# The first expert's choice as a job of its own, the sorting in three pieces, the last block's gathers first

## The chip, the cores and the metric

The kernel runs on one core of a Trainium2 chip. The metric is the device time of one execution in microseconds, as the median of the runs shown. The engines are PE (TensorE's matmuls), DVE (VectorE), ACT (ScalarE), POOL (GpSimd) and SP (SyncE, which issues most of the DMAs). Each works through its own queue of instructions in the order in which the program emits them.

## The reference

One layer of a decoder block on 1024 tokens of width 1024, in float32. A mixer (stick-breaking attention and a gated linear recurrence, each projected, gated and merged, then an output projection), a layer norm, a mixture of experts, and a layer norm again:

```
h = layer_norm(alpha * x + mixer(x))              # the mixer ends in merged @ w_out
logits = h @ router_w + router_b                  # 32 experts
top 4 of 32 for each token, gates = softmax of the four
per expert: hcat = h_rows @ w_up[e] + b_up[e]     # 1024 -> 2048, even columns gate, odd linear
            act = min(glu, 7) * sigmoid(1.702 * glu) * (clip(lin, -7, 7) + 1)
            y = act @ w_down[e] + b_down[e]       # 1024 -> 1024
out = layer_norm(alpha * h + sum over the four of gate * y)
```

Only the rows that chose an expert go through it. Which rows these are is known when all 1024 tokens have been routed.

## The kernel before

Products that must keep float32 accuracy are done as three matmuls on a high and a low part of each operand (`split` makes the parts: ACT casts the high one, DVE or POOL subtracts for the low one). The kernel projects the input, runs the recurrence and the attention, merges both branches, and then comes to the part that the change touches, `outproj` and the start of `experts`.

**`outproj`** works on eight blocks (tb) of 128 tokens. `project` (L955) multiplies a block of the merged branches by `w_out`, which lies in the slots `raw0` to `raw5`, `wh0`, `wl0`, `wh1`, `wl1`: 48 matmuls in two halves into two PSUM banks called `mix`. `add` (L948) adds the residual for a half and takes its statistics; after both halves `layer_norm` (L890) makes h of the block on DVE, in four instructions of 512 columns, and h is stored to `h_scratch`. `route(tb)` (L1049) does the block's routing in pieces, each ending in a `yield`: transposes of h (L1057) and their copies on ACT, the router product (L1064), the logits and the top four and gates on DVE (L1069 to L1108), `spread` (L1099, the gates over the 32 experts), then `place` (L983: how many earlier tokens chose each expert, a running sum `macc` in L989), the row numbers (L1117 to L1123), four indirect DMAs on POOL that write token and gate into the table `tab_scratch` (L1130), then the biases' product with the gates (L1148 to L1160), whose result is stored as the start of the accumulator.

The order is written out by hand. A loop (L1169 to L1183) goes through the pieces of `project`, two of the eight products of a half at a time; each piece is a step. After each step, every routing job in `live` makes one piece. Blocks 0 and 1 take 16 steps together, later ones 8 each; a block's routing begins `LAG` = 5 steps after its projection. The last two pieces of block 7 have no step.

**The first expert** does not wait for the full routing. After block `CHOOSE` = 4, `choose` (L1011) takes the expert with the fewest tokens so far, keeps its number in `e0` (by which SP loads its weights) and marks which tokens of the blocks so far chose it, as 128 by 128 squares S of zeros and ones (`chosen`, L996). After block 5 `fetch_chosen` (L1034) makes the token numbers from S (L1040) and gathers these rows of h from `h_scratch` by an indirect DMA (L1046). The rows of blocks 6 and 7 are added on PE: `gather` (L1005) multiplies h by S into the two banks `x0`, on top of the fetched rows, so that the first expert's input stands there transposed, never having gone through memory. `choose` and `fetch_chosen` are called inside `route` by `yield from`, so that the block's own scatters come behind them.

**The tail** (L1185 to L1211) brings routing of blocks 6 (`side`) and 7 (`last`) to their ends in an order of its own, with `until(g, what)` running one up to a named point: m is the mask of a block, s its squares, x its gather, g its gates, p its scatters. `sort_experts` (L1233) counts each expert's tokens and sorts the experts by them, giving `eid`, the list by which all further weights are loaded.

**`experts`** (L1607) runs the 32 experts. Each piece of an expert's two products has a weight load (SP, into one of six `raw` slots of 1 MB), a `part` (the split into one of eight `wh`, `wl` pairs; every fifth is POOL's) and the matmuls. Loads are emitted `RLOOK` = 14 pieces ahead and parts `LOOK` = 6 ahead. The first expert multiplies its first 512 columns whole (L1524, from the copy `xf` of its input in `wh5`), its others in parts (L1511). What is left of the routing stands in the list `side`, up to two pieces for each piece of the first expert. Expert 1's rows are gathered by POOL (L1354) after `enter` has loaded its places; PE transposes them (L1390) at the first piece of expert 1. `bank` (L168) gives the PSUM banks in turn, four `mix` and two `sm`. Experts whose capacity is over 128 are wide (18 of them), the others narrow (14).

`scratch` (L232) runs early and fills the DRAM scratch, the rows of `h_scratch` with zeros that no store has reached when they are read.

Of the kernel before, what the change touches and what calls it, by code (L numbers as in the profile page):

```python
# [42 lines left out]
LAG = 5  # L43
HOLD = 3
STILL = 2
CHOOSE = 4
POOLED = 5
ORD = (("s", 0), ("s", 1), ("s", 2), ("s", 3), ("s", 4), ("c", 0, 2, "p"), ("a", 0, "pp", "pp"), ("s", 5), ("s", 6), ("a", 1, "pp", "pp"), ("c", 2, 6, "v"), ("s", 7), ("c", 6, 8, "v"), ("a", 2, "xx", "xx"), ("a", 3, "xx", "vv"), ("a", 4, "pv", "vv"), ("a", 6, "pp", "pv"), ("a", 5, "vp", "vv"), ("a", 7, "vp", "vv"))
LOOK = 6
# [98 lines left out]
class Block:  # L148
# [19 lines left out]
    def bank(self):  # L168

        i = self.turns.get("bank", 0)  # L170
        self.turns["bank"] = (i + 1) % 6
        return self.fps.tile([128, 512], F32, name="mix" if i < 4 else "sm", bufs=4 if i < 4 else 2)

    def dram(self, name, shape, dtype=F32):
        return self.nc.dram_tensor(name, shape, dtype).ap()
# [56 lines left out]
    def scratch(self):  # L232

        nc = self.nc
        self.tab_d = self.dram("tab_scratch", (NE * ROWS, 2), I32)
        self.h_d = self.dram("h_scratch", (ROWS, D))
        self.acc_d = self.dram("acc_scratch", (ROWS, D))
        n = NE * ROWS // 128
        for i in range(2):
            t = self.work.tile([128, n], I32, name="E0", bufs=EBUFS[0])  # L240
            nc.sync.dma_start(t, self.a["c_tab"][:, n * i:n * i + n])
            nc.gpsimd.dma_start(self.tab_d.rearrange("(p r) c -> p (r c)", p=128)[:, n * i:n * i + n], t)
        z = self.work.tile([128, 512], F32, name="E0", bufs=EBUFS[0])
        nc.gpsimd.memset(z, 0.0)
        for d in (self.h_d, self.acc_d):
            for half in range(2):
                nc.gpsimd.dma_start(d[T:T + 128, 512 * half:512 * half + 512], z)

        for half in range(2):
            nc.gpsimd.dma_start(self.h_d[T - 128:T, 512 * half:512 * half + 512], z)  # L250


    def load_x(self):
# [636 lines left out]
    def layer_norm(self, pool, r, st, g, b, out):  # L890

        nc = self.nc
        mv = pool.tile([128, 2], F32, name="mv", bufs=2)
        nc.vector.bn_aggr(mv, st)
        y = self.rsqrt(pool, mv[:, 1:2], 1.0, LN_EPS, 1)
        for op0, k, op1, v, to in ((OP.subtract, mv[:, 0:1], OP.mult, g, r), (OP.mult, y, OP.add, b, out)):
            for half in range(2):
                s = slice(512 * half, 512 * half + 512)
                nc.vector.scalar_tensor_tensor(to[:, s], r[:, s], k, v[:, s], op0=op0, op1=op1)

    def outproj(self):
# [53 lines left out]
        def project(tbs):  # L955

            for tb in tbs:
                W["ps", tb] = [self.fps.tile([128, 512], F32, name="mix", bufs=4) for _ in range(2)]
                W["r", tb] = self.residual[:, tb % 2]
            todo = [(tb, half, k) for tb in tbs for half in range(2) for k in range(KT)]  # L960
            if len(tbs) > 1:
                todo.sort(key=lambda x: x[2])
            for i, (tb, half, k) in enumerate(todo):
                mh, ml = (p[k // 4][:, k % 4, 128 * (tb % 2):128 * (tb % 2) + 128] for p in self.mt[tb // 2])
                n = slice(512 * half, 512 * half + 512)
                o = W["ps", tb][half]
                wh, wl = self.wo[k]
                nc.tensor.matmul(o, mh, wh[:, n], start=k == 0, stop=False)
                nc.tensor.matmul(o, mh, wl[:, n], start=False, stop=False)
                nc.tensor.matmul(o, ml, wh[:, n], start=False, stop=k == KT - 1)  # L970
                if k == KT - 1:
                    add(tb, half)
                    if half and tb + 2 < NB:
                        load_x(tb + 2)
                if i % 2 and i + 1 < len(todo) or i + 2 == len(todo):
                    yield
            for tb in tbs:
                h = self.at(HSLOTS[tb], [128, D], F32)
                self.layer_norm(lk, W["r", tb], W["st", tb], ln_g, ln_b, h)
                nc.gpsimd.dma_start(self.h_d[128 * tb:128 * tb + 128], h)  # L980
                W["h", tb] = h

        def place(tb, m):  # L983

            pr = self.fps.tile([128, 512], F32, name="sm", bufs=2)
            nc.tensor.matmul(pr[:, :NE], self.before, m, start=True, stop=False)
            nc.tensor.matmul(pr[:, :NE], self.ones, macc, start=False, stop=True)
            nc.vector.scalar_tensor_tensor(mr[:, tb], pr[:, :NE], 1.0, m.bitcast(F32), op0=OP.add, op1=OP.mult)
            nc.vector.tensor_add(macc, macc.bitcast(F32), m.bitcast(F32))  # L989
            if tb > CHOOSE + 1:  # L990
                chosen(tb, tb + 1)
                yield "s"
                gather(W["h", tb], S[tb], False, tb == NB - 1)
                yield "x"
# [15 lines left out]

        def choose():  # L1011

            yield
            ps = self.fps.tile([128, 512], F32, name="sm", bufs=2)
            nc.tensor.matmul(ps[:, :NE], self.ones, macc, start=True, stop=True)
            neg = wk.tile([128, NE], F32, name="lg", bufs=2)
            nc.vector.tensor_scalar(neg, ps[:, :NE], -1.0, None, op0=OP.mult)
            mx = wk.tile([128, 8], F32, name="mx", bufs=2)
            mi = wk.tile([128, 8], U32, name="mi", bufs=2)
            nc.vector.max(mx, neg)  # L1020
            nc.vector.max_index(mi, mx, neg)
            ef = wk.tile([128, 4], F32, name="idf", bufs=2)
            nc.vector.tensor_copy(ef, mi[:, :4])
            nc.vector.tensor_scalar(oe, self.iota_e, ef[:, :1], None, op0=OP.is_equal)
            self.e0 = self.epool.tile([1, 1], I32, name="e0")
            nc.vector.tensor_copy(self.e0, ef[:1, :1])
            self.ch0 = self.epool.tile([128, 1], F32R, name="ch0")
            nc.vector.memset(self.ch0[2 * NE:].bitcast(F32), 0.0)
            nc.vector.tensor_scalar(self.ch0[:2 * NE], self.ecol, ef[:2 * NE, :1], None, op0=OP.is_equal)
            self.squares = self.at("wl2", [128, NB, 128], F32)  # L1030
            chosen(0, CHOOSE + 1)
            yield

        def fetch_chosen():  # L1034

            chosen(CHOOSE + 1, CHOOSE + 2)
            yield
            ps = self.fps.tile([128, 512], F32, name="sm", bufs=2)
            for tb in range(CHOOSE + 2):
                nc.tensor.matmul(ps[:, :2], S[tb], self.tokf[:, tb:tb + 2], start=tb == 0, stop=tb == CHOOSE + 1)  # L1040
# [8 lines left out]
        def route(tb):  # L1049
            h = W["h", tb]  # L1050
            hT = self.at("wl4", [128, D], F32).rearrange("p (k t) -> p k t", t=128)
            for g in range(2):
                last = tb == NB - 1
                p = self.fps.tile([128, 512], F32, name="mix" if last else "ht", bufs=4 if last else 2)
                p = p.rearrange("p (k t) -> p k t", t=128)
                for i in range(4):
                    nc.tensor.transpose(p[:, i], h[:, 128 * (4 * g + i):128 * (4 * g + i) + 128], self.idn)  # L1057
# [64 lines left out]
            idx = wk.tile([128, 4], I32, name="idx", bufs=2)  # L1122
            nc.vector.tensor_copy(idx, ds_)  # L1123
            if tb == CHOOSE:
                yield from choose()
            if tb == CHOOSE + 1:
                yield from fetch_chosen()
            for k in range(4):
                nc.gpsimd.memset(self.spacer, 0.0)
                s = nc.gpsimd.indirect_dma_start(  # L1130
# [4 lines left out]
                scat.append(s)  # L1135
            if late:
                yield "p"
                if tb == NB - 1:
                    self.sort_experts(oe)
                    yield "o"  # L1140
                spread()
            else:
                for _ in range(HOLD):
                    yield
# [42 lines left out]
        def until(g, what):  # L1187
            while next(g) != what:
                pass
# [1 line left out]
        side = live.pop()  # L1191
        next(side)
        until(side, "m")
        next(last)
        self.x0 = [self.fps.tile([128, 512], F32, name="mix", bufs=4) for _ in range(2)]
        gather(self.xg[0], self.idn, True, False)
        next(last)
        until(side, "s")
        until(last, "m")
        until(side, "x")  # L1200
        until(last, "s")
        until(last, "x")
        yield
        for g in (side, last):
            until(g, "g")
            until(g, "p")
        yield
        until(last, "o")
        yield
        for g in live + [side, last]:  # L1210
            yield from g  # L1211


# [19 lines left out]
    def sort_experts(self, first):  # L1233
# [2 lines left out]
        ps = self.fps.tile([128, 512], F32, name="sm", bufs=2)  # L1236
        nc.tensor.matmul(ps[:NE, :NE], self.ones[:, :NE], self.macc, start=True, stop=True)
        nc.tensor.matmul(ps[:NE, 32:34], self.macc, self.ones[:, :2], start=True, stop=True)

        key = cp.tile([NE, NE], F32, name="key")  # L1240
        nc.vector.scalar_tensor_tensor(key, ps[:NE, :NE], 32.0, c32[:, 0], op0=OP.mult, op1=OP.add)
# [10 lines left out]
        nc.vector.tensor_reduce(pos, key, axis=AX.X, op=OP.add)  # L1252
        perm = cp.tile([NE, NE], F32, name="perm")
        nc.vector.tensor_scalar(perm, c32[:, 3], pos, None, op0=OP.is_equal)
        ps = self.fps.tile([128, 512], F32, name="sm", bufs=2)
        for i in range(2):
            nc.tensor.matmul(ps[:1, 32 * i:32 * i + 32], ec[:, i:i + 1], perm, start=True, stop=True)
# [349 lines left out]
    def experts(self, routing):  # L1607
# [76 lines left out]
            call(t)  # L1684
        fetch(10)
        next(routing)
        next(routing)
        nc.gpsimd.memset(self.xg[1], 0.0)
        for i in range(LOOK):
            part(i)  # L1690
        soon, side, listing = [], [], None
        side += [("r", lambda: next(routing, None))] * 28

        def due(ts):

# [4 lines left out]

        for i, (q, kind, j) in enumerate(order):
            part(i + LOOK)
            fetch(i + RLOOK)
            if kind == "down" and j == 0:
                due([t for t in soon if t[1] == q])
            if kind == "up" and j == 0 and q:
# [274 lines left out]
```

## Time and profile before

| | |
|---|---|
| median of 3 runs | 2585.21 us (2582.81 to 2588.27) |
| profiled execution | 2587.85 us |
| its span, first to last instruction | 2586.3 us |
| mean granted TensorE clock | 0.972 |
| PE, PEld | 94%, 84% of the span busy |
| DVE, ACT, POOL | 72%, 58%, 34% |
| DMA | 551.18 MB, mean 213 GB/s |

The projection of the output and the routing run from about 875 to 1034 us, the first expert from 1043, and the experts up to about 2500. In the rows below a line number is that of the kernel, a tile's name is that of the place it lies in (a small routing tile carries the name of the slot it is cut from: `aTA`, `gl`, `yT`, `wl`). An engine's idle time before an instruction stands in brackets with what ended it. The granted clock is 1.00 at 2.4 GHz and 0.50 at 1.2 GHz, and a stretch's mean lies between.

### The profile page before, as it was taken

To read this page: it belongs to the slowest core of one execution; us is meant where nothing else is said; L and a number is where in the kernel's file an instruction comes from. 1 tells how busy PE (TensorE), PEld (TensorE's weight loads), DVE (VectorE), ACT (ScalarE), POOL (GpSimd) and SP (SyncE) were. 2 spreads that over 40 slices of the span, in tenths; PEclk is the share of its full clock that TensorE was granted. 3 is DMA by queue.
4 is the path that set the end of the run, shared out by engine and by line. 5 is a ranking of instruction groups with operands and counts; after the bars stand their busy time and mean duration, and the time that the engine had idled before them with its cause. 6 is when DMAs were issued, how large, how long until landed. Compare 5 with 4: busy or idle time off the path is not lost. (4 is left out here: it accounts for less than half of the span.)

```text
span 2586.3 us, 42032 instructions
## 1 busy us (share of the span) xinstructions
PE 2438.3 (94%) x15521; PEld 2177.2 (84%) x15521; DVE 1865.0 (72%) x3160; ACT 1491.7 (58%) x2558; POOL 878.0 (34%) x751
## 2 busy tenths in 40 slices
PE   8999999989979987799999999999999999999992
PEld 8898888887867765599999999999899899899892
DVE  3216674338884575688878788988888888889885
ACT  3213332327664311477777777777777777777772
POOL 1011011004331232344444443444444444454443
PEclk9999999999989998899999999999999999999996
DMA  5321243223324524789899899997999989999963
GB/s 164 107 80 56 68 121 102 66 50 94 87 82 147 162 91 159 232 270 300 288 308 307 258 305 293 322 317 259 307 313 315 303 270 324 309 304 319 319 208 139
DMA packets 429703, 551.18 MB, mean 213 GB/s; under 512 B 21079, under 2 KB 316135, under 8 KB 429493
## 3 DMA queue, kind: packets, MB, share of 16 engines
q1 hardware_dynamic: 407284, 480.42, 57.2%
q0 software_dynamic: 22208, 68.03, 9.2%
q8 instruction: 123, 2.02, 0.3%
q14 instruction: 88, 0.71, 0.1%
HBM read 496.40 MB, written 51.99 MB: 212 GB/s over the span
## 5 line engine op out<-in xcount | busy, mean ns | idle before, releaser
L181 DVE TENSOR_TENSOR wl<-raw,wh 128x1024 fp32r<-128x1024 f32 x668 | 872.2, 1320 | 194.5 <-ACT wh L180 190.9
L180 ACT CAST wh<-raw 128x1024 fp32r<-128x1024 f32 x820 | 867.2, 1079 | 60.3 <-PE pj L332 20.6
L181 POOL TENSOR_TENSOR wl<-raw,wh 128x1024 fp32r<-128x1024 f32 x152 | 376.8, 2479 | 488.9 <-ACT wh L180 455.1
L1427 PE MATMUL mix<-xTA,wh 128*128 128x292 f32 (+16 forms) x1504 | 390.8, 346 | 0.0
L1429 PE MATMUL mix<-xTA,wl 128*128 128x146 f32 (+16 forms) x1504 | 354.0, 235 | 0.0
L1429 PEld LDWEIGHTS mix<-xTA,wl 128*128 128x128 f32 x1504 | 287.5, 191 | 0.5
L1427 PEld LDWEIGHTS mix<-xTA,wh 128*128 128x128 f32 x1504 | 282.8, 188 | 0.6
L1427 PE MATMUL sm<-xTA,wh 128*128 128x292 f32 (+16 forms) x800 | 213.9, 350 | 0.0
L185 PE MATMUL pj<-xh,wh 128*128 128x512 f32 x512 | 208.1, 406 | 0.0
L181 POOL TENSOR_TENSOR aTA<-gl,aTA 128x146 fp32r<-128x146 f32 (+16 forms) x144 | 112.7, 784 | 278.5 <-ACT aTA L180 261.8
L1477 PE MATMUL mix<-aTA,wh 128*128 128x292 f32 (+16 forms) x680 | 203.9, 347 | 0.0
L187 PE MATMUL pj<-xh,wl 128*128 128x512 f32 x512 | 201.4, 393 | 0.0
L186 PE MATMUL pj<-xl,wh 128*128 128x512 f32 x512 | 201.0, 393 | 0.0
L1429 PE MATMUL sm<-xTA,wl 128*128 128x146 f32 (+16 forms) x800 | 189.3, 237 | 0.0
L1479 PE MATMUL mix<-aTA,wl 128*128 128x146 f32 (+16 forms) x680 | 160.2, 236 | 0.0
L1429 PEld LDWEIGHTS sm<-xTA,wl 128*128 128x128 f32 x800 | 154.0, 193 | 0.0
L1427 PEld LDWEIGHTS sm<-xTA,wh 128*128 128x128 f32 x800 | 151.6, 190 | 0.2
L1477 PE MATMUL sm<-aTA,wh 128*128 128x292 f32 (+16 forms) x472 | 148.5, 345 | 3.1 <-POOL aTA L181 3.1
L1511 PE MATMUL mix<-wh,xTB 128*128 128x512 f32 x336 | 144.3, 430 | 0.0
L1513 PE MATMUL mix<-wh,xTB 128*128 128x512 f32 x336 | 133.4, 397 | 0.0
L1512 PE MATMUL mix<-wl,xTB 128*128 128x512 f32 x336 | 133.0, 396 | 0.0
L1479 PEld LDWEIGHTS mix<-aTA,wl 128*128 128x128 f32 x680 | 130.0, 191 | 0.0
(481 smaller groups left out, 5680.6 us busy)
## 6 DMA issues: line engine op xcount, KB each, us to landing
raw<-in_expert_w_up_dram SPq DMA_DIRECT2D x256, 1024.0 KB
raw<-in_expert_w_down_dram SPq DMA_DIRECT2D x128, 1024.0 KB
raw<-in_w_in_dram SPq DMA_DIRECT2D x56, 512.0 KB
gate_scratch<-pe POOLq DMA_DIRECT2D x32, 256.0 KB
gate<-gate_scratch SPq DMA_DIRECT2D x8, 1024.0 KB
qf<-in_x_dram SPq DMA_DIRECT2D x8, 512.0 KB
qraw<-q_scratch SPq DMA_DIRECT2D x16, 256.0 KB
wh<-in_x_dram SPq DMA_DIRECT2D x8, 512.0 KB
```

Of the source, the lines that this page charges most:

```text
L180: nc.scalar.copy(hi, src)
L181: (engine or nc.vector).tensor_tensor(lo, src, hi.bitcast(F32), op=OP.subtract)
L185: nc.tensor.matmul(ps, wh, xh, start=start, stop=False)
L186: nc.tensor.matmul(ps, wh, xl, start=False, stop=False)
L187: nc.tensor.matmul(ps, wl, xh, start=False, stop=stop)
L1427: nc.tensor.matmul(ps[g][:, :2 * n], wh[:, kk, 128 * g:128 * g + 128], x[k].rearrange("p a n -> p (a n)"), start=k == 0, stop=False)
L1429: nc.tensor.matmul(ps[g][:, :n], wl[:, kk, 128 * g:128 * g + 128], x[k][:, 0], start=False, stop=k == KT - 1)
L1477: nc.tensor.matmul(ps[i][:, :2 * n], wh[:, kk, s], act[:, k].rearrange("p a n -> p (a n)"), start=k == 0, stop=False)
L1479: nc.tensor.matmul(ps[i][:, :n], wl[:, kk, s], act[:, k, 0], start=False, stop=k == KT - 1)
L1511: nc.tensor.matmul(p, x[k][:, 0], wh[:, kk], start=k == 0, stop=False)
L1512: nc.tensor.matmul(p, x[k][:, 0], wl[:, kk], start=False, stop=False)
L1513: nc.tensor.matmul(p, x[k][:, 1], wh[:, kk], start=False, stop=False)
```

## The change

`CHOOSE` becomes 3 and `WAIT` = 4 is new. `choose` and `fetch_chosen` are no longer called inside a block's routing but go into `live` as jobs of their own, which let four steps pass before they begin. The fetched rows are now those of blocks 0 to 4, and block 5 joins 6 and 7 in being added on PE; its squares are made in its `place`, its gather is in the tail. The zero rows of `h_scratch` cover the last two blocks. The four `mix` banks are named one by one, with a ring of one each. The layer norm does both operations of one half, then of the other. In the tail, what is left of block 5's routing is run to its end, and the gathers of the fetched rows and of block 5 come before the transposes of block 7. `sort_experts` yields twice: its counts come at the end of the tail, its chain on DVE after the scatters of blocks 6 and 7, its last piece (the sorted list) three pieces later, among those of the first expert. Then `spread` of block 6 and of block 7 have a piece each before the biases' products.

```diff
-CHOOSE = 4
+CHOOSE = 3
+WAIT = 4
...
-        return self.fps.tile([128, 512], F32, name="mix" if i < 4 else "sm", bufs=4 if i < 4 else 2)
+        return self.mix((i + 2) % 4) if i < 4 else self.fps.tile([128, 512], F32, name="sm", bufs=2)
+
+    def mix(self, i):
+        return self.fps.tile([128, 512], F32, name=f"mix{i}", bufs=1)
...
-        for half in range(2):
-            nc.gpsimd.dma_start(self.h_d[T - 128:T, 512 * half:512 * half + 512], z)
+        for tb in range(NB - 2, NB):
+            for half in range(2):
+                nc.gpsimd.dma_start(self.h_d[128 * tb:128 * tb + 128, 512 * half:512 * half + 512], z)
...
-        for op0, k, op1, v, to in ((OP.subtract, mv[:, 0:1], OP.mult, g, r), (OP.mult, y, OP.add, b, out)):
-            for half in range(2):
+        for half in range(2):
+            for op0, k, op1, v, to in ((OP.subtract, mv[:, 0:1], OP.mult, g, r), (OP.mult, y, OP.add, b, out)):
...
-                W["ps", tb] = [self.fps.tile([128, 512], F32, name="mix", bufs=4) for _ in range(2)]
+                W["ps", tb] = [self.mix(2 * (tb % 2) + i) for i in range(2)]
...
             if tb > CHOOSE + 1:
                 chosen(tb, tb + 1)
+                if tb < NB - 2:
+                    return
                 yield "s"
                 gather(W["h", tb], S[tb], False, tb == NB - 1)
...
         def choose():
-            yield
+            for _ in range(WAIT):
+                yield
...
             chosen(0, CHOOSE + 1)
-            yield
 
         def fetch_chosen():
             chosen(CHOOSE + 1, CHOOSE + 2)
-            yield
+            for _ in range(WAIT):
+                yield
...
-                p = self.fps.tile([128, 512], F32, name="mix" if last else "ht", bufs=4 if last else 2)
+                p = self.mix(2 + g) if last else self.fps.tile([128, 512], F32, name="ht", bufs=2)
...
             if tb == CHOOSE:
-                yield from choose()
+                live.append(choose())
             if tb == CHOOSE + 1:
-                yield from fetch_chosen()
+                live.append(fetch_chosen())
...
             if late:
                 yield "p"
-                if tb == NB - 1:
-                    self.sort_experts(oe)
-                    yield "o"
                 spread()
...
         until(side, "m")
-        next(last)
-        self.x0 = [self.fps.tile([128, 512], F32, name="mix", bufs=4) for _ in range(2)]
+        for g in live:
+            drain(g)
+        self.x0 = [self.mix(i) for i in range(2)]
         gather(self.xg[0], self.idn, True, False)
+        gather(W["h", NB - 3], S[NB - 3], False, False)
         next(last)
         until(side, "s")
+        next(last)
         until(last, "m")
         until(side, "x")
         until(last, "s")
         until(last, "x")
+        sort = self.sort_experts(oe)
+        next(sort)
         yield
         for g in (side, last):
             until(g, "g")
             until(g, "p")
+        next(sort)
+        for _ in range(3):
+            yield
+        drain(sort)
         yield
-        until(last, "o")
-        yield
-        for g in live + [side, last]:
+        for g in (side, last):
+            next(g)
+            yield
+        for g in (side, last):
             yield from g
...
         nc.tensor.matmul(ps[:NE, 32:34], self.macc, self.ones[:, :2], start=True, stop=True)
+        yield
...
         nc.vector.tensor_scalar(perm, c32[:, 3], pos, None, op0=OP.is_equal)
+        yield
...
         next(routing)
-        next(routing)
         nc.gpsimd.memset(self.xg[1], 0.0)
...
-        side += [("r", lambda: next(routing, None))] * 28
+        side += [("r", lambda: next(routing, None))] * 40
...
-            fetch(i + RLOOK)
+            fetch(i + RLOOK if i > 1 else count(0))
```

## Rows read from the trace of the kernel before

**Rows 1.** Waits of PE from 1108 to 2500 us: total, times, longest.

```profile
PE ht L1549 <- DVE gl L1541: 7.0, 9, 2.3
PE sm L1477 <- POOL aTA L181: 2.3, 4, 1.4
```

**Rows 2.** Busy time by stretch: length, engines, granted clock, DMA share, GB/s.

```profile
970.00:1020.00 50.00, 34.70 (x168) 27.14 (x166) 30.62 (x103) 5.55 (x18) 14.71 (x26) 0.80 0.36 121
...
1053.00:1090.00 37.00, 28.77 (x122) 22.65 (x120) 26.63 (x43) 19.49 (x27) 11.33 (x10) 0.83 1.00 322
...
1032.00:1040.00 8.00, 2.09 (x18) 2.00 (x18) 4.09 (x16) 2.38 (x8) 0.31 (x1) 0.99 0.00 1
```

**Rows 3.** Waits of PE from 967 to 1092 us.

```profile
PE sm L1257 <- DVE perm L1254: 8.2, 1, 8.2
PE sm L1015 <- DVE gl L989: 7.5, 1, 7.5
PE sm L1040 <- DVE wl L1003: 5.9, 1, 5.9
PE sm L1148 <- DVE yT L1103: 5.2, 2, 3.3
PE mix L1057 <- DVE yo L899: 2.2, 1, 2.2
...
PE ht L1390 <- DMA xg<-h_scratch,ti: 1.8, 1, 1.8
```

**Rows 4.** Waits of DVE from 967 to 1092 us.

```profile
DVE xTB L952 <- PE mix L970: 8.8, 2, 6.4
DVE aTA L1071 <- PE sm L1069: 5.8, 1, 5.8
DVE wl L181 <- ACT wh L180: 5.1, 3, 4.1
...
DVE gl L1534 <- PE mix L1530: 3.2, 1, 3.2
```

**Rows 5.** DVE in order of time: start, us, operation, [idle before <-releaser].

```profile
983.14 0.18 DVE L1017 TENSOR_SCALAR aTA<-sm 128x32 f32<-128x32 f32 x1
...
986.60 0.67 DVE L952 SCALAR_TENSOR_TENSOR xTB<-wh,mix 128x512 f32<-128x512 f32 x1
...
993.77 0.19 DVE L1071 TENSOR_TENSOR aTA<-sm,aTA 128x32 f32<-128x32 f32 x1 [5.77 <-PE sm L1069]
...
1001.89 1.41 DVE L899 SCALAR_TENSOR_TENSOR yo<-xTB,gl,aTA 128x512 f32<-128x512 f32 x2
...
1017.56 0.69 DVE L952 SCALAR_TENSOR_TENSOR xTB<-wh,mix 128x512 f32<-128x512 f32 x1 [6.39 <-PE mix L970]
...
1043.94 4.63 DVE L181 TENSOR_TENSOR wl<-raw,wh 128x1024 fp32r<-128x1024 f32 x4
```

**Rows 6.** PE in order of time, merged.

```profile
983.12 0.63 PE L969 MATMUL mix<-wl,xTA 128*128 128x512 f32 x1
...
1014.47 0.48 PE L968 MATMUL mix<-raw,xTA 128*128 128x512 f32 x1
...
1017.13 0.40 PE L970 MATMUL mix<-wh,xTA 128*128 128x512 f32 x1
...
1032.39 2.05 PE L1008 MATMUL mix<-wl,yo 128*128 128x128 f32 x16 [1.05 <-DVE wl L1003]
...
1034.31 0.17 PE L1238 MATMUL sm<-gl 128*32 128x2 f32 x1
...
1042.98 5.49 PE L1524 MATMUL mix<-raw,wh 128*128 128x512 f32 x8
...
1049.50 3.60 PE L1524 MATMUL mix<-raw,wh 128*128 128x512 f32 x8
```

**Rows 7.** POOL in order of time.

```profile
156.21 0.54 POOL L388 DMA_DIRECT2D hv_scratch<-pe  x1 [83.88 <-DVE pe L387]
...
1073.04 1.15 POOL L1354 DMA_INDIRECT xg<-h_scratch,ti  x1 [0.33 <-DMA ti<-tab_scratch]
```

## The prediction

> **What bounds the kernel now.** I read first the waits of PE in the long expert stage, then how busy the engines are in the stretches before it, then the waits of PE and of DVE there, and last the order of work inside them. The reader is to see four things.
>
> From 1108 to 2500 us PE waits 9.3 us in all [rows 1]: the expert stage runs at PE's pace, so whatever lets PE enter it earlier is kept to the end.
>
> Before that stage PE is not full: 34.7 us busy of 50 from 970 to 1020, at a granted clock of 0.80, and 28.8 of 37 from 1053 to 1090, at 0.83 [rows 2]. Between 967 and 1092 its three longest waits are all for DVE: 8.2 us at L1257 (the sorting), 7.5 at L1015 (the choice), 5.9 at L1040 (the list of chosen rows) [rows 3].
>
> DVE waits for PE in the same stretch: 8.8 us in two waits at L952 (the halves of the last block), 5.8 at L1071 (a block's logits), 3.2 at L1534; and 4.1 at L181 for a cast of ACT's, which stands until L1524 has read `wh5` [rows 4]. So neither engine is the bound here. Each stands in turn because its next instruction is queued behind something late, and that is slack which an order can take out.
>
> The transfers are no bound just then either: from 1032 to 1040 their share is 0.00 [rows 2], since the six `raw` slots are full and only L1524 frees the first.
>
> **The choice and the list, moved to other steps.** Counting as the loop does, blocks 0 and 1 take steps 0 to 15 and each later block eight; `place` of block 3 falls in step 41, of block 4 in 49, of block 5 in 57. Before, the choice is in step 50, one step behind `place(4)`, whose sum DVE writes last of all that is queued: 7.5 us. After, it is in step 46, five steps behind `place(3)`; the list is in step 54, five behind `place(4)`, in place of step 58, one behind `place(5)`.
>
> DVE's work stays nearly the same in sum. Choice and squares of five blocks are 983.14 to 986.60 [rows 5], 3.5 us; with four squares about 3.2, and the fifth alone in step 50 about 0.7, which is 0.4 more. So DVE ends `place(4)` not at 983.14 but 3.2 later, at 986.3, the square at 987.0, and stands before `add(6, 0)` at the time it does now. What changes is behind that: PE has not stood for 7.5 us. Of DVE's waits, 5.8 + 8.8 = 14.6 are then open to go, less the 0.4: 14.2.
>
> PE's side must allow it, and there two waits stay: for the layer norm of block 5 and for the square of block 4, 987.0. Behind the square come L1040, the router product, the last product of block 6 and L1069, some 3.2 us of short PE work, so that L1071 of block 5 starts at 990.2, now 993.77. From there to the end of block 6's layer norm the same DVE instructions follow as now, 993.77 to 1001.89 + 1.41 [rows 5], 9.5 us: 999.7. Then the second half of block 6's transposes, 0.4, and the last 12 product matmuls, 1014.47 to 1017.53 now [rows 6], 3.1. `add(7, 1)` would start at 1003.1, where it starts at 1017.56 now: **14.5 us**, and the two ways agree within 0.3. I take 1.0 off for the clock. After a long wait the matmuls take 0.63 us, at the full clock 0.40 [rows 6], for some 14 of them: 3.2 us a time. The waits that stay are of 2 to 3 us and may cost none or all of one such stretch, 0 to 3.2; partly covered by DVE, hence 1.0.
>
> The Trainium skill, "TensorE: Matmul & The Clock Gate", Part 1, says that the throttled level is the default and that activity releases it. By that alone the waits that stay would bring the low level back and the sum would lose the 3.2. The clock of 0.80 agrees for waits of 6 and 7 us; no row shows what waits as short as the new ones do.
>
> The scatters of blocks 3 and 4 move with `place` and no longer stand behind the choice on POOL; the gather of the listed rows goes out some 14 us ahead of its use, as now. SP has only the load of `x` and then the weights there, which wait for the projection to free the `raw` slots and come forward with it. Nothing is late there. The two added zero stores are two POOL issues of 0.54 us early in the run, and POOL waits 83.88 us before 156.21 [rows 7]: nothing.
>
> **The last block's chain.** PE gets one more set of gather matmuls (block 5; a set takes 2.05 us [rows 6]), and the gathers of the fetched rows and of block 5, 4.1 to 4.8 us, stand before the transposes of block 7. Their cover is PE's 2.2 us at L1057 [rows 3] and the time behind the router product; the transposes come some 2 us later than they could, but L1064 of block 7, now behind the gather of the fetched rows, no longer waits for that. The layer norm's halves in the other order give the first half 0.7 us sooner and make each second instruction depend on the one before. Without its cover the block would cost its 2.05 us; if all of it hides and the half order tells, 1.0 is won. I take nothing. The bias products of block 5, drained here, are two short DVE instructions in a wait of DVE for PE: nothing.
>
> **The sorting in three pieces.** Now L1257 stands in PE's queue ahead of the first expert matmul and waits 8.2 us for DVE, which has the gates of two blocks and the sorting's chain to do. L1524's own inputs are there: PE's last work is at 1034.31, L1524 starts at 1042.98 [rows 6]. After, L1257 stands behind both products of the first column group, 5.49 + 3.60 us [rows 6], by when the permutation is ready. So L1524 starts 8.2 us sooner relative to the last block. What hangs on it follows: the cast that waits for `wh5`, so DVE's 4.1, and then the 3.2.
>
> `eid` comes later, behind up to six of DVE's splits, each 1.16 us (four are 4.63 [rows 5]): some 7 us. SP's loads of expert 1 and of the first down weights are queued behind it; they are wanted some 25 us later, after three more column groups. If that cover were gone it would cost these 7.
>
> The bounds: below, POOL, whose scatters, memset, split and stores lead to the gather for expert 1 at 1073.04 [rows 7], for which PE waits [rows 3]; if only DVE's 4.1 comes through to it, 4.1. Above, the wait for the spread gates, L1148, goes as well: 8.2 + 5.2 = 13.4. I take **8.2**, the wait itself, near DVE's 4.1 + 3.2.
>
> The sum: 14.5 - 1.0 + 0 + 8.2 = **21.7 us**. The profiled execution took 2587.85 us (span 2586.3), 0.1% over the median of the runs; 2587.85 - 21.7 = 2566.2, and carried to the median 2585.21 - 21.7 = **2563.5 us**. The forecast stands for gains of 17 to 28 us, 2557 to 2568.
>
> **The rivals.**
>
> *Only part of it arrives.* The low clock takes 3.2 in both places, or the tail is held by the gather for expert 1: issued at 1073.04, it still keeps PE waiting with the DMA share at 1.00 from 1053 to 1090 [rows 2]. Against: those loads are spread over a longer time once they start sooner. Gains of 8 to 17 us, 2568 to 2577. The Trainium skill, "DMA: Bandwidth & Descriptors", section Queues, rings and completion order, says that each engine takes turns between the queues that have work; by it an earlier gather would still share with weight loads, which move forward too, and land as slowly as now.
>
> *More than the sum.* The clock of 0.83 from 1053 to 1090 is a third of the stretch at half speed; if PE stays fast there, up to 5 us more, and with the tail's upper bound another 5: gains of 28 to 36, 2549 to 2557. Against: PE still meets waits of several us.
>
> *No change.* The weights' stream sets the pace, so that PE starts sooner only to wait. For it: that share of 1.00. Against: the 9.3 us [rows 1], and that the stream itself restarts as soon as L1524 frees a slot. Within 5 us of 2585.
>
> *Slower.* The four `mix` banks become four rings of one, and the rotation through them goes on for all experts: 18 wide ones with 24 turns and 14 narrow ones with 6, 516 turns. If a turn now waits longer for its bank, the price is 516 times that; from 42 ns a turn it eats the 21.7 us, and at 80 ns the kernel is at 2605. Against: the six banks still come round in turn, and PE's waits in that stage name no reader of a bank [rows 1].
>
> **How the numbers follow.** Forecast 0.62, part only 0.16, more 0.10, no change 0.06, slower 0.06. Faster by over 0.2% (5.2 us, about what a measurement of this kernel tells from no change) are the first three: 0.88; within it 0.06; slower 0.06. The range takes the forecast whole, most of the part case and half of the larger one: 2553 to 2576.
>
> **What would show it.** Right: L1015 and L1040 gone from PE's long waits or below 3 us; the last L952 near 1003; L1524 directly behind L1238 and ahead of L1257; the pause of the transfers between the first six loads and the next some 6 us and not 16; the gather for expert 1 some 20 us earlier. Wrong: a new wait of PE over 6 us at L1057, L1148 or L1390 in those 90 us; a last L952 after 1010; for the slower case, waits of PE at its `mix` products in the expert stage.

## The result and the profile after

The changed kernel takes 2571.52 us (median of 4 runs, 2568.91 to 2572.76), beside 2586.43 us of the kernel before in the same session: ratio 0.9943, interval 0.9926 to 0.996, so 14.7 us faster by the ratio (the medians lie 14.9 apart). Run again later it gave 2568.36 us, ratio 0.9934 [0.992, 0.9948], 17.1 us by the ratio. The forecast was 2563.5, with 2557 to 2568 for its own case. The first result lies outside that, in the range of the rival by which only part of the gain arrives, and inside the range of all cases together, 2553 to 2576. The profiled execution has a span of 2569.3 us, 17.0 under that of before.

The expert stage is untouched, as its waits from 1108 to 2500 us show beside [rows 1]:

```profile
PE ht L1566 <- DVE gl L1558: 7.0, 9, 2.3
PE sm L1494 <- POOL aTA L185: 2.3, 4, 1.4
```

So nearly all of it lies ahead of that stage. First the stretches of [rows 2], then PE's waits from 967 to 1092 us, beside [rows 3]:

```profile
970.00:1020.00 50.00, 41.77 (x276) 32.99 (x274) 41.06 (x140) 7.65 (x23) 18.41 (x33) 1.00 0.57 189
1053.00:1090.00 37.00, 30.23 (x136) 25.17 (x136) 25.48 (x30) 20.88 (x31) 13.86 (x9) 0.86 0.86 267
1032.00:1040.00 8.00, 2.87 (x9) 1.84 (x8) 7.81 (x17) 4.70 (x7) 7.33 (x7) 0.51 0.36 109
```

```profile
PE sm L1153 <- DVE yT L1111: 5.1, 1, 5.1
PE ht L1407 <- DMA xg<-h_scratch,ti: 3.8, 1, 3.8
PE sm L991 <- DVE yT L1092: 2.8, 1, 2.8
PE ht L1566 <- DVE gl L1558: 2.6, 1, 2.6
...
PE sm L1274 <- DVE perm L1270: 1.0, 1, 1.0
```

The waits of 7.5 and 5.9 us for the choice and the list are gone, and that of 8.2 for the sorting is 1.0 (L1257 is now L1274). From 970 to 1020 PE is busy for 41.8 us, where it was 34.7, at the full clock of 2.4 GHz (those 50 us now hold work that stood some 10 us later in the kernel before). From 1032 to 1040 PE is still mostly idle, but DVE and POOL are now full. PE in order of time (start, us), the last product of the projection first:

```profile
1006.60 0.40 PE L975 MATMUL mix<-wh,xTA 128*128 128x512 f32 x1
...
1022.09 0.17 PE L1253 MATMUL sm<-gl 128*32 128x2 f32 x1
1022.12 7.11 PE L1541 MATMUL mix<-raw,wh 128*128 128x512 f32 x16
...
1030.50 0.27 PE L1274 MATMUL sm<-perm,ec 32*1 32x32 f32 x4 [1.03 <-DVE perm L1270]
...
1070.70 1.76 PE L1407 MATMUL ht<-idn,xg 128*128 128x128 f32 x7 [3.80 <-DMA xg<-h_scratch,ti]
```

The first expert's products stand directly behind L1253, 20.9 us earlier than in [rows 6]. But the gather for expert 1 (POOL, L1371) is only 15.2 us earlier than in [rows 7], and PE waits 3.8 us for it. DVE and POOL between:

```profile
1007.03 0.69 DVE L957 SCALAR_TENSOR_TENSOR xTB<-wh,mix 128x512 f32<-128x512 f32 x1 [0.41 <-PE mix L975]
...
1030.37 5.75 DVE L185 TENSOR_TENSOR wl<-raw,wh 128x1024 fp32r<-128x1024 f32 x5
...
1043.62 4.01 DVE L185 TENSOR_TENSOR wl<-raw,wh 128x1024 fp32r<-128x1024 f32 x1
```

```profile
1027.48 1.01 POOL L1138 DMA_INDIRECT tab_scratch<-aTA  x1 [10.73 <-DVE aTA L1098]
...
1031.37 5.59 POOL L1138 DMA_INDIRECT tab_scratch<-aTA  x1 [0.22 <-issue]
...
1041.30 1.91 POOL L1138 DMA_INDIRECT tab_scratch<-aTA  x1 [0.22 <-issue]
...
1044.12 2.41 POOL L185 TENSOR_TENSOR wl<-raw,wh 128x1024 fp32r<-128x1024 f32 x1
...
1057.85 1.21 POOL L1371 DMA_INDIRECT xg<-h_scratch,ti  x1 [1.40 <-DMA ti<-tab_scratch]
```

One of the eight scatters of blocks 6 and 7 takes 5.59 us, the others 0.96 to 1.91. In the kernel before these are the first, the two longest, which stand beside a run of four splits of DVE's, and the last:

```profile
1039.69 0.98 POOL L1130 DMA_INDIRECT tab_scratch<-aTA  x1 [15.43 <-DVE aTA L1090]
...
1044.79 1.21 POOL L1130 DMA_INDIRECT tab_scratch<-aTA  x1 [0.22 <-issue]
...
1046.30 1.97 POOL L1130 DMA_INDIRECT tab_scratch<-aTA  x1 [0.22 <-issue]
...
1049.85 0.97 POOL L1130 DMA_INDIRECT tab_scratch<-aTA  x1 [0.22 <-issue]
```

### The profile page after: what moved, and what is told of

Same layout as the page of the kernel before. It is cut to its first block, busy times and chain, and to the rows that moved or that the text cites. A ratio compares the mean times of both kernels' runs of the same rounds, so it can differ in the third digit from the quotient of the medians.

```text
span 2569.3 us, 42071 instructions
## 1 busy us (share of the span) xinstructions
PE 2430.6 (95%) x15535; PEld 2171.0 (84%) x15535; DVE 1873.2 (73%) x3162; ACT 1492.3 (58%) x2558; POOL 881.0 (34%) x753
```

## The experiments

Each profile gives five marks: the first product of the projection with the low part of the tokens (the first L975, half a microsecond behind the first of all), the last addition (L957), the first product of the first expert (L1541), the first issue of the gather for expert 1 (L1371), the first down product of the first expert. P, A, G and D are the four times between them, in us; the gain is the kernel before's median less this one's by the ratio, in that session.

| | P | A | G | D | gain | ratio and interval |
|---|---|---|---|---|---|---|
| before | 142.2 | 25.4 | 30.1 | 23.9 | | |
| changed (first) | 128.9 | 15.1 | 35.7 | 22.5 | 14.7 | 0.9943 [0.9926, 0.996] |
| e1 choice alone | 125.3 | 27.2 | 29.4 | 21.4 | 15.0 | 0.9942 [0.9928, 0.9956] |
| e2 sorting alone | 139.3 | 16.6 | 35.5 | 22.0 | 7.0 | 0.9973 [0.9965, 0.9982] |
| e3 chain undone | 125.6 | 18.3 | 35.3 | 23.0 | 17.1 | 0.9934 [0.9921, 0.9948] |
| e4 changed again | 128.7 | 15.1 | 35.5 | 22.8 | 17.1 | 0.9934 [0.992, 0.9948] |
| e5 late loads | 128.7 | 15.1 | 35.9 | 22.9 | 15.2 | 0.9941 [0.9927, 0.9954] |
| e6 splits off POOL | 127.3 | 16.7 | 36.6 | 22.8 | 15.8 | 0.9939 [0.9926, 0.9953] |
| e7 earlier gather | 127.3 | 16.7 | 33.5 | 22.2 | 19.1 | 0.9926 [0.9912, 0.9939] |
| e8 three together | 128.0 | 15.1 | 35.7 | 20.7 | 19.6 | 0.9924 [0.991, 0.9937] |
| e9 one step's wait | 138.3 | 16.7 | 35.6 | 22.5 | 6.5 | 0.9975 [0.9963, 0.9986] |
| e10 e7, early pieces | 130.6 | 16.7 | 31.2 | 20.9 | 19.1 | 0.9926 [0.991, 0.9943] |
| e11 e10, old norm order | 128.4 | 15.1 | 31.2 | 20.8 | 19.6 | 0.9924 [0.9907, 0.9941] |
| e12 e11, no early pieces | 129.2 | 15.1 | 33.4 | 20.9 | 18.1 | 0.993 [0.9915, 0.9945] |

P is not steady: with the same order of work it was 127.3 to 130.6 (changed, e4 to e8, e10), with the norm's old order and the new choice 125.3 to 129.2 (e1, e3, e11, e12), with the old choice 142.2 and 139.3 (before, e2), and the stages ahead of it, alike in all but two stores, ended anywhere from 872.7 to 878.1 us. A of 16.7 in place of 15.1 is a draw of the clock: the clock granted over A is 0.90 in e6, e7, e9 and e10 and 1.00 in the changed kernel, e4 and e12. The stretch of A in e7, in the changed kernel and, for what follows, in e3 (columns as in [rows 2], the clock third from the end):

```profile
1000.02:1016.74 16.72, 13.12 (x117) 11.89 (x116) 11.09 (x38) 2.66 (x8) 4.24 (x8) 0.90 1.03 356
```

```profile
1007.03:1022.12 15.09, 11.54 (x116) 10.32 (x117) 11.03 (x38) 2.65 (x8) 4.24 (x8) 1.00 1.01 343
```

```profile
999.43:1017.70 18.27, 12.94 (x116) 11.61 (x116) 10.82 (x38) 2.75 (x8) 4.23 (x8) 0.91 1.02 367
```

G and D repeat within 0.4 from the changed kernel to e4. D does not always: between e7 and e12, which differ only ahead of the last block, it varies by 1.3, and between the kernel before and e1 by 2.5.

**The parts of the change (e1 to e4).** e1 has the moved choice alone and e2 the split sorting alone, both without the chain's order and the norm's and with the old single ring of `mix` banks. e3 is the changed kernel with those two orders undone:

```diff
+        next(last)                     # ahead of gather(self.xg[0], ...), in place of further down
-        for half in range(2):
-            for op0, k, op1, v, to in (...):
+        for op0, k, op1, v, to in (...):
+            for half in range(2):
```

> Before, with only the choice and the list moved (CHOOSE 3, WAIT 4, block 5 added on PE); sorting whole and ahead of the first product, tail and layer norm as before. Theory A (two slacks that add): the last L952 comes 13 to 14 us sooner, the tail behind it keeps its length, so 12 to 14 us faster than before. Theory B (the tail's gather for expert 1 bounds both): nearly all of the changed kernel's gain is in here, 15 to 17 us. Theory C (the choice only helps together with the sorting): under 6 us.

> Before, with only the sorting in three pieces (block 5's rest drained in the tail as it needs); choice as before after block 4. Theory A: the first product L1524 follows directly on the last block, 8 to 10 us sooner relative to it, of which the gather for expert 1 passes on 4 to 6: 4 to 6 us faster. Theory B: 0 to 2 us, since POOL's chain to that gather starts from the scatters and not from L1524. If the whole 8 arrived: 8 to 10.

> The changed kernel with the last block's chain put back: transposes of block 7 ahead of the gathers, layer norm by operation and not by half. Theory A (costs and gains nothing): within 2 us of the changed kernel, 14 to 19 us faster than before. Rival: the 1.7 us by which the last gather came sooner behind L952 is this part's, and is lost: 2 us slower than the changed kernel.

> The changed kernel once more, on the same chip as the other three, for a narrower interval: profile says 17.0 us of span, the medians 14.9. Theory A: 15 to 18 us faster than before. Also: does the scatter of 5.59 us on POOL, while five splits run without a gap on DVE, come again? By the theory that DVE and POOL hinder each other it does, 3 to 6 us long; if it was chance, all scatters are at 0.9 to 2.0 us.

e1 gains in P (142.2 to 125.3) and keeps the wait for the sorting. Its gain of 15.0 lies just inside theory B, but A, G and D together stay near their length (79.4 to 78.0), as theory A says and B does not. e2 gains in A (25.4 to 16.6) and keeps the two waits for the choice, and in it G grows by 5.4. A, G and D together fall by 5.3, inside theory A's 4 to 6; the time gains 7.0, between theory A and the whole 8. The scatter that is held is in e2 too (5.57 us), and in e4 (5.58), so it comes with the split sorting and is no chance. PE's waits of e1, then of e2:

```profile
PE sm L1263 <- DVE perm L1260: 8.2, 1, 8.2
```

```profile
PE sm L1015 <- DVE gl L989: 7.5, 1, 7.5
PE sm L1040 <- DVE wl L1003: 5.9, 1, 5.9
```

The two gains add to 22, and e3, which has both, gains 17.1; with intervals of 2 to 4 us on each side the shortfall of 5 is not proved by the times. The chain's order seems to take 3.2 us out of A (18.3 in e3 to 15.1), but e3 had the lower clock there: beside the kernels that have the order and the same granted clock (16.7) it is 1.6. Block 5's added gather costs 1.7 to 1.8 (16.6 to 18.3 from e2 to e3, 25.4 to 27.2 from the kernel before to e1), so the two cancel. e3 is not slower than e4, whose P is 3.1 longer. Whether the norm's order costs P anything is not settled, since the values of P for the two orders overlap.

**One step in place of four (e9).**

```diff
-WAIT = 4
+WAIT = 1
```

> The changed kernel with the two jobs of the choice (the sum of the counts, and the list of the chosen expert's tokens) one step after their block in place of four; the block that is chosen by stays the earlier one. Theory D (the deferral by steps carries the gain: TensorE no longer stands at a product whose operand VectorE has not made yet): the waits of 7.5 and 5.9 us of the kernel before come back nearly whole, the last addition falls 9 to 13 us later than in the changed kernel, and the time is 8 to 13 us above the changed kernel's. Rival B (choosing by an earlier block carries it, the steps do little): the time is the changed kernel's within 3 us.

Two waits of PE return, 3.5 us for the choice and this one for the list:

```profile
PE sm L1048 <- DVE wl L1010: 5.7, 1, 5.7
```

P is back at 138.3, near the 139.3 and 142.2 of the old choice, and the gain is 6.5 us, about the 7.0 that the split sorting gives by itself. Theory D holds by the time and by the list's wait; the wait for the choice came back only half. (With `WAIT` = 1 each job runs two steps behind its block's `place`, where it was one in the kernel before.) Choosing by an earlier block is worth nothing alone that these times show; the steps of delay are.

**Who holds up the scatter (e5, e6).** e5 puts SP's wait for the sorted list ahead of the loads of the fourth column group; e6 gives the first expert's pieces all to DVE.

```diff
+            if i == 2:
+                get(1)
-            fetch(i + RLOOK if i > 1 else count(0))
+            fetch(i + RLOOK if i > 1 else 10)
```

```diff
-            self.split(wh, wl, r, nc.gpsimd if self.pieces % POOLED == 0 else nc.vector)
+            self.split(wh, wl, r, nc.gpsimd if self.pieces % POOLED == 0 and not first else nc.vector)
```

> The changed kernel with one move: SyncE reads the first list entry's expert (its wait for the sorted list) ahead of the loads of the first expert's fourth chunk, so that these loads no longer run beside the last two blocks' scatters. In the changed kernel one scatter on GpSimd takes 5.6 us at 1031 us, beside DMA traffic and beside five VectorE splits back to back; in the kernel before none is above 2.0 us. Theory L (the weight loads hold the scatter up): the longest scatter falls under 2.5 us, the gather for expert 1 is issued about 3 to 4 us sooner, and the time is 2 to 4 us under the changed kernel. Theory V (VectorE's five splits hold it up): it stays at 5 us or more and the time is within 2 us of the changed kernel or up to 5 us above it, because the fourth chunk comes later and TensorE waits for it.

> The changed kernel with the first expert's weight splits all on VectorE, none on GpSimd (three pieces move). In the changed kernel three operations of VectorE take 4.0, 4.9 and 2.9 us beside GpSimd's splits, against 0.4 to 1.2 us elsewhere. Theory G (what GpSimd has to do ahead of the gather for expert 1, and what it does to VectorE meanwhile, sets when expert 1 begins): these three fall to their usual length, the gather is issued 1 to 3 us sooner, and the time is 1 to 3 us under the changed kernel. Rival P (TensorE's own queue sets it): VectorE has three more splits of about 1.2 us, TensorE waits for them, and the time is the changed kernel's within 1 us, or up to 4 us above it.

In e5 the scatter is as long as before, in a stretch in which the transfers stand at 0.01; POOL's row, then the stretch:

```profile
1026.89 5.58 POOL L1138 DMA_INDIRECT tab_scratch<-aTA  x1 [0.21 <-issue]
```

```profile
1026.90:1032.50 5.60, 1.91 (x5) 1.00 (x5) 5.60 (x9) 4.59 (x6) 5.60 (x2) 0.59 0.01 2
```

Theory L falls: the loads do not hold the scatter. In e6 DVE's run has six splits, and the scatter has grown with it:

```profile
1026.01 6.88 DVE L185 TENSOR_TENSOR wl<-raw,wh 128x1024 fp32r<-128x1024 f32 x6
```

```profile
1027.03 6.71 POOL L1138 DMA_INDIRECT tab_scratch<-aTA  x1 [0.22 <-issue]
```

DVE's operations of 4.0, 4.9 (two splits) and 2.9 us are gone as theory G said, but the gather is 0.9 us later after the first product and not 1 to 3 sooner: the scatter's hold is 1.1 us longer. The time is the changed kernel's, as rival P had it.

**The gather and the early pieces (e7, e8, e10 to e12).** e7 issues the gather two pieces sooner; e8 is e6 and e7 and the bias products six steps later in place of one; e10 is e7 with two pieces split ahead of the first expert's tokens; e11 is e10 with the norm by halves in the last block alone; e12 is e11 without the early pieces.

```diff
-            if (q, kind, j) == (0, "up", 4):
+            if (q, kind, j) == (0, "up", 2):
...
-                if j == (GJ if q else 6):
+                if j == (GJ if q else 4):
```

```diff
         next(routing)
+        fetch(10)
+        part(2)
+        part(3)
         for t in get(0)["turns"]:
             call(t)
-        fetch(10)
...
-        for i in range(LOOK):
+        for i in range(4, LOOK):
```

> The changed kernel with the gather for expert 1 issued two chunks of the first expert sooner (after its fifth up chunk in place of the seventh), the read of the expert's row list with it. Theory G (this gather sets when expert 1 begins; in the changed kernel TensorE waits 3.8 us for it before its first transposes): the gather is issued 4 to 8 us sooner, the wait goes, and the time is 2 to 4 us under the changed kernel; more than the 3.8 us can't come from it. Rival P (TensorE's own queue, or the list itself, sets it): the gather waits for the list or TensorE for something else as long, and the time is the changed kernel's within 1 us.

> The changed kernel with the two edits of the runs on GpSimd's splits and on the earlier gather together, and the last two blocks' bias products six steps later in place of one, so that TensorE no longer waits 5.1 us for VectorE's spread there. If the tail gives back what the two halves of the change lose together (15 and 7 us alone, 17 together) in these three places, the time is 5 to 10 us under the changed kernel, near 2559 to 2563 us in this run's terms. If TensorE's waits there only change places, it is within 2 us of the better one of the two single edits.

> The kernel with the earlier gather for expert 1, and beside it the first two pieces of the first expert's weights split ahead of its own tokens' split, in VectorE's idle time of 2.4 us there, so that its burst of five splits beside the scatters becomes three. Theory V (a scatter can't go on while VectorE's splits run back to back): the longest scatter falls from 5.6 to about 3.4 us (the burst of three), all behind it on GpSimd comes 2 us sooner, VectorE's cast of the sorted list 2.3 us sooner, TensorE's wait of 5.7 us at the bias transposes falls to about 3.4 us, and the time is 1 to 3 us under that kernel's (19 us under the kernel before as first measured, so 20 to 22 now). Rival N (the scatter's length goes by its phase against the splits, not by their number): it stays near 5 us or falls to 2 us at once; the gain by TensorE's wait stays.

> The previous kernel (earlier gather, two early pieces) with the layer norm half by half for the last block alone; blocks 0 to 6 take both halves of one operation, then of the other, as in the kernel before. From the run with the tail's order undone, where blocks 4 to 7 took 43.3 us in place of 44.4, the order by halves costs about 1 us over four blocks and 2 us over seven, and gains in the last block alone. Expected: 1 to 2 us under the previous kernel, some 21 to 24 us under the kernel before. If the order of the halves costs nothing: the same within 0.5 us.

> The previous kernel without the two early pieces: the earlier gather, and the layer norm half by half for the last block alone. It separates the two edits. Theory V: a scatter of 5.6 us again, and 1 to 3 us above the kernel with both. If the early pieces gain nothing: the same within 0.5 us.

In e7 PE's wait for the gather is gone and G is 2.2 shorter, not 4 to 8 as theory G had it, because the gather now waits for the row list:

```profile
1050.20 1.00 POOL L1371 DMA_INDIRECT xg<-h_scratch,ti  x1 [5.64 <-DMA ti<-tab_scratch]
```

The gain is 19.1, 2.0 over the changed kernel's 17.1 with overlapping intervals, so the times do not settle it. Part of it went into two new waits, for a piece that POOL splits behind the gather and for DVE, which stood 5.86 us at one small operation beside POOL's splits; PE's waits, then DVE's row:

```profile
PE mix L1529 <- POOL wl L185: 2.9, 1, 2.9
PE ht L1407 <- DVE xTA L185: 2.8, 1, 2.8
```

```profile
1053.17 5.86 DVE L1558 SCALAR_TENSOR_TENSOR gl<-gl 128x256 f32<-128x256 f32 x1 [0.15 <-ACT gl L1557]
```

In e8 the wait of 5.1 at L1153 fell to 0.7 and one of 5.9 came at the gate's transposes behind it, so the waits changed places, as the rival said.

e10 shortens DVE's run to three splits, and the scatter follows:

```profile
1029.02 3.47 DVE L185 TENSOR_TENSOR wl<-raw,wh 128x1024 fp32r<-128x1024 f32 x3
```

```profile
1030.04 3.30 POOL L1138 DMA_INDIRECT tab_scratch<-aTA  x1 [0.21 <-issue]
```

Theory V holds by 3.30, 5.59 and 6.71 us for three, five and six splits: the scatter ends 0.8 to 0.9 us behind the last split each time. In all three it began 1.0 us into the run, so the number of splits was varied and the start was not. G is 2.2 shorter in e11 than in e12, as the scatter is (5.58 to 3.31). PE's wait at L1153 fell only to 4.2, not 3.4. The times don't follow clearly: e10 was to be 20 to 22 us under the kernel before and is 19.1, e11 1 to 2 under e10 and is 2.0 by its median (2563.58 to 2565.60) in overlapping intervals, e12 1.7 over e11, likewise.

e11 beats the kernel before clearly. Against the changed kernel its tail (A, G and D together) is 6.3 us shorter, 67.1 to 73.4, but the ratios, 0.9924 [0.9907, 0.9941] and 0.9934 [0.992, 0.9948], don't tell the two apart.

## Why the prediction came out as it did

**The choice and the list: right, and the size in part by luck.** 14.5 less 1.0 were forecast; P fell by 13.3, and by 13.5 in the second profile. The last addition stood at 1007.03; its 4 us over the forecast 1003 are mostly the 2.8 by which this execution was late at the first projection product. That the size agrees within 0.2 us is chance, since P varies by some 3 us from one execution to the next. The reason was the right one: e9 takes most of the delay away and loses the gain. The working by steps of the loop is what gave it. Not all of the 13.3 is waiting. In the stretch of P, here from the very first product on, before and then after,

```profile
874.85:1017.56 142.71, 120.54 (x593) 93.57 (x595) 95.09 (x283) 26.58 (x64) 46.15 (x79) 0.89 0.36 120
```

```profile
877.62:1007.03 129.41, 114.95 (x592) 88.98 (x594) 96.38 (x285) 27.02 (x65) 43.82 (x75) 0.96 0.38 126
```

PE's idle time falls by 7.7 us. Its busy time falls by 5.6 for the same work (593 and 592 instructions), with a granted clock of 0.96 where it was 0.89.

**The clock: nothing was lost there in this execution.** The 1.0 for a second stretch at half speed did not come: waits of up to 2.8 us stand in the stretch from 970 to 1020 and its granted clock is 1.00. The same order of work shows 0.97 over that stretch in e4 and e5 and 0.93 in e6 and e7, so this was the draw of one execution; e4:

```profile
970.00:1020.00 50.00, 42.92 (x277) 34.68 (x276) 41.30 (x140) 7.64 (x23) 18.38 (x34) 0.97 0.58 197
```

What that costs does not show in P (128.7 in e4, 127.3 in e7), and the 1.0 is neither confirmed nor refuted. The prediction takes the sentence of the Trainium skill's "TensorE: Matmul & The Clock Gate", Part 1, to mean that such waits bring the low level back. In the changed kernel's first profile they did not, in e4 one of 3.0 us was followed by it. Later in the first profile the clock falls to 0.50 just after 1032, ahead of the wait of 5.1 us (1033.7 to 1038.8) and with PE busy for most of the time until then:

```profile
1022.00:1032.00 10.00, 8.53 (x29) 3.90 (x28) 7.79 (x32) 5.96 (x11) 3.86 (x7) 1.00 0.86 289
1032.00:1034.00 2.00, 1.70 (x5) 0.83 (x3) 2.00 (x3) 2.00 (x3) 2.00 (x1) 0.54 0.95 337
```

So that long wait did not start the low level, in which the matmuls take 0.63 us on both sides of it.

**The last block's chain: nothing, as taken**, and as the working had it: block 5's gather costs 1.7 to 1.8 us in A (2.05 without its cover) and the new order gives 1.6 back at the same clock.

**The sorting: the mis-sized term.** 8.2 us were taken between bounds of 4.1 and 13.4. PE's part came out near that: A fell by 8.8 in e2, which has this part alone, and by 10.3 in the changed kernel, where some 1.6 is the clock's. L1541 stands behind L1253. But expert 1 starts from its gather. From the last addition to the gather the time fell from 55.5 to 50.8, 4.7 us, and D by 1.4: 6.0 in all. By the rows of POOL the 4.7 has three parts. From the last addition to the first of the eight scatters it is 22.1 before and 20.4 after. The eight scatters take 11.1 before and 15.7 after. From the end of the last to the gather it is 22.2 before and 14.6 after. So 7.6 us come free behind the scatters and 1.7 ahead of them, and 4.6 are lost within them, which is the scatter that is held; e2 shows the same two large parts (7.8 and 4.6). The step that failed is that the tail's term let POOL's scatters keep their length. That the split sorting would put a run of five splits beside them was not in the working, though the prediction counted up to six of them ahead of the cast of the sorted list; that count was right, SP waits 7.3 us for it, some 7 forecast. That a hold passes on to the gather is shown by e11 beside e12: 2.3 us less hold, 2.2 less in G. No run has the split sorting without any hold, so that the whole 8.2 would then arrive is not shown. The 4.7 is near the lower bound, "if only DVE's 4.1 comes through", by chance: more came through, and part of it was lost again.

So of 21.7 forecast, 13.3 + 6.0 + 0.4 (the experts) = 19.7 are in the profile, and 2.8 went the other way ahead of the change, where only two stores differ and where executions vary by 5. Of D's 1.4 some may be chance as well, since e1, with the old tail, has D at 21.4. The rival "only part of it arrives" came out by its number; of its two causes the low clock did not take 3.2 in P, and the gather for expert 1 did keep PE waiting (3.8 us). The first result lies in its range, and the second at its edge.

**The signs.** L1015 and L1040 are gone from PE's long waits, L1541 stands directly behind L1253 and ahead of L1274, and no wait at L1065, L1153 or L1407 is over 6 us. The transfers, which stood still for some 17 us before (about 1032 to 1049), stop for about 1 us near 1026 and again for some 4.5 from 1034 on, where SP waits for the sorted list. The last addition came at 1007 and not 1003, and the gather for expert 1 15.2 us earlier and not 20.

**The other rivals** did not come. PE names no reader of a `mix` bank in the expert stage, whose two waits are the same to a tenth, so the rings of one bank cost nothing that shows; from the first down product to the end it is 1487.4 to 1489.3 us in the three kernels with one ring of four (before, e1, e2) and 1487.0 to 1489.6 in those with four of one. The gather's landing, from its second issue to PE's start, was 12.0 us before (1074.49 to 1086.45) and 11.3 after (1059.36 to 1070.70), so an earlier gather landed about as slowly as before, as the sentence on the queues would have it. That turns between queues are the reason, no run tests.

## What to carry to other kernels

When two engines stand for each other by turns, count in which step of the written order each result is ready, and move the reader a few steps on; this was worth about 13 us here and was foretold by counting, within the 3 us by which executions vary. When a wait of the busy engine goes, price what follows by the chain that feeds the next stage, not by the wait that went: 8.8 us came free at PE in e2, and 3.4 arrived at the gather. Look at what fills the engines in the freed time, since a run of VectorE's operations may now lie beside GpSimd's; here that took back 4.6 us.

## What the runs showed of the hardware

A scatter on GpSimd that began 1.0 us into a run of back-to-back VectorE splits (128x1024, two operands in SBUF) ended only behind the last of them: 3.3, 5.6 and 6.7 us for 3, 5 and 6 splits, where most others took 1.0 and none over 2.0. The other way round, single operations of VectorE that usually take 0.4 to 1.2 us took 2.9 to 5.9 beside one or two of GpSimd's splits of 2.4 us. The Trainium skill, "SBUF — State Buffer", section SBUF: two separate sides, states that the two engines share one pair of ports as an exclusive lock (for a VectorE operation with two inputs in SBUF, against a GpSimd operation that reads SBUF), held for a whole instruction, and that the loser stands still. The runs agree in that one engine stands while the other works; that this lock is the cause in a scatter, no run tests. What they add is that a scatter stood for a run of several instructions, not for one. Two kernels do not fit, the one before and e1: in each, two scatters got through a run of four splits in 1.2 and 1.97 us. Why is open; in all the kernels in which one was held it starts 1.0 us after the run, in these two 0.85, and no run varies that start alone.
